# Gating norm and inverse merges cut into smaller pieces, and the later adaLN modulations moved from the chain stage into the projection stage

## The chip, the cores and the metric

The kernel runs on one core of a Trainium2 chip. The metric is the device time of one execution in microseconds. The engines named below: PE (TensorE, matrix products), DVE (VectorE), ACT (ScalarE), POOL (GpSimd) and SP (SyncE, here the queue that issues most transfers).

## The reference, cut to what matters

Two layers work on 512 latent tokens and 256 context tokens of width 1024. Each sub-layer is a norm, a modulation from a conditioning vector (adaLN), a mixer, a norm, a gate and a residual. In the first layer the mixer is a spatial-gating MLP (4 groups) beside a bidirectional RWKV-7 (8 heads), both fed by one projection; the second layer's mixer is an mLSTM; a ConvFFN follows each.

```
def ada_mod(cvec, w, b):                       # w: 1024 x 6144, six vectors of 1024
    m = jax.nn.silu(cvec) @ w + b
def spatial_gate(p, w_s, b_s, g_v):
    u, v = jnp.split(jax.nn.gelu(p[..., :2 * A_WIDTH]), 2, axis=-1)
    v = rmsnorm(v.reshape(bn, t // CHUNK, CHUNK, A_GROUPS, A_GDIM), g_v)
    z = jnp.einsum('gpq,bnqgc->bnpgc', w_s, v) + b_s.T[None, None, :, :, None]
    return u * z.reshape(bn, t, A_WIDTH)
def rwkv7_scan(r, w, k, v, kk, b, s0):
    def step(s, inp):
        sa = jnp.einsum('bhvk,bhk->bhv', s, kk_t)
        s = s * w_t[:, :, None, :] - sa[..., None] * b_t[:, :, None, :] + v_t[..., None] * k_t[:, :, None, :]
        return s, jnp.einsum('bhvk,bhk->bhv', s, r_t)
```

## The kernel before, in words

The change touches the first layer's mixer alone. It is written in three parts.

*Norm and first projections.* The tokens are normed, transposed and modulated with the first two modulation vectors (`ada_0`); the result `hT` is kept as a high and a low half. A matrix product of full precision is three passes: weights high by input high, weights high by input low, weights low by input high.

*Projection stage.* A *unit* is one 128-column tile of the input projection: `load_w` fetches 512 KB of weights into one of two `raw` slots (`strm.raw` is 2), ACT writes the high half, POOL the low half (two buffers each), and `proj_pass` runs 24 passes over the 512 latent tokens and 24 over the 256 context tokens, into PSUM banks 0 and 1. There are 23 units: three for the low-rank inputs, then k, r and v for four tiles `ct` of the RWKV part (`kr`, `v`) and u and v for four groups of the gating part (`sgu`). For every `ct`, `prep_e` makes the decays and key products, `prep_n` the 64x64 matrices of each chunk, and `prep_t` their triangular inverses: a scan of 31 steps on DVE (L597, L599) over 32x32 blocks, then transposes `Td`, `Tn`, `On`, copies on ACT (L613, L614), and two merges on PE (L621 with the ACT copy L624, L630 with the DVE copy L633). The gating norm in `sgu` transposes v on PE (L822), squares it on ACT (L826), takes the power on POOL (L827, L828), multiplies on DVE (L829), multiplies with the spatial weights on PE (L833) and evicts on DVE (L837, L841).

*Chain stage.* The four tiles are written to and read back from HBM, and the chunk recurrence runs as two interleaved lanes over a pair of tiles (`lane`, `chains`), with the next inputs (`preps`), the inverses of tiles 2 and 3 (`Ts`) and the finishing norms beneath it, in six blocks `b`. The remaining modulations of the first layer that need the matrix `ada_w` (`ada_job([1, 2])`: vectors 2, 3 and 4) are computed in blocks 2 to 4 as well: `ada_gen` loads a slab of weights and multiplies it with the two conditioning vectors, in column tiles of 32 of the array (L157), all sums in PSUM bank 7; at the end the sums are copied (L162), transposed (L165) and added to the bias (L169). The result is read first in the gate of the output projection that follows.

All generators are merged by `weave`: a piece is what lies between two `yield`s, a generator with weight n and offset f has its i-th piece at the key f + (1 − f)(i + 0.5)/n, and the smallest key comes next:

```
k = min(range(len(live)), key=lambda j: live[j][3] + (1 - live[j][3]) * (live[j][1] + 0.5) / live[j][2])
```

`part_of(g, n)` takes n pieces of a generator, `part(n)` n pieces of the gating groups. The order so written is the priority for the framework's planner, which sets the order on each engine and puts in the waits; each engine, and the SP queue, then works strictly in its order. The projection stage has three rounds, `ct` = 0, 1, 2: in round `ct` the inverse of tile `ct` (in round 2 the first seven pieces of tile 2's inverse) is woven with `prep_e` and `prep_n` of tile `ct + 1`, and with its v, the k and r of tile `ct + 2` and `NA[ct]` pieces of the gating groups.

Of the kernel before, what the change touches and what calls it, by code (L numbers as in the profile page):

```python
# [74 lines left out]
def _build(ctx, tc, xall, par, cst, ada_0, ada_w, ada_t, w_in, w_out, ffn_up, ffn_down, lora, wsT, a_bs, c_in, c_gate, c_out, mneg, parf, parm, out):  # L75
# [33 lines left out]
    class strm:  # L109
        pool, rawp, raw, hi, lo = None, None, 2, 2, 2  # L110
# [33 lines left out]
    def ada_gen(g, pool, tag, rawb, cols=1024, rtag="araw", width=None):  # L144

        n = min(2048, 5120 - g * 2048)
        width, cols = width or cols, min(cols, n)
        m = n // 512
        pb = bank(f"ada_{g}", tag)
        for kt in range(KT):  # L150
            for c0 in range(0, n, cols):
                pl = pool[(c0 // cols) % len(pool)] if isinstance(pool, list) else pool
                raw = pl.tile([P, width], F32, tag=rtag, name=f"ada{g}{kt}{c0}", bufs=rawb)[:, :cols]
                nc.sync.dma_start(raw, ada_w[kt, :, (g - 1) * 2048 + c0:(g - 1) * 2048 + c0 + cols])
                for q2 in range(cols // 512):
                    q = c0 // 512 + q2
                    nc.tensor.matmul(pb[32 * q:32 * q + 32, :], silu[:, kt, :],  # L157
                                     raw[:, q2 * 512:(q2 + 1) * 512],
                                     start=(kt == 0), stop=(kt == KT - 1))
            yield  # L160
        sb = (pool[0] if isinstance(pool, list) else pool).tile([P, width], F32, tag=rtag, name=f"adasb_{g}", bufs=rawb)[:, :512]
        V.tensor_copy(sb[:32 * m], pb[:32 * m])  # L162
        pt = bank(f"adat_{g}", tag)
        for j in range(4):
            nc.tensor.transpose(pt[:, j * 128:j * 128 + 32 * m], sb[:32 * m, j * 128:(j + 1) * 128], ident[:32 * m, :32 * m])  # L165

        o = PC.at["ada_b0"][0]
        for cnd in range(2):
            V.tensor_tensor(mod[0][:, cnd, g * 16:g * 16 + 4 * m].rearrange("p (q j) -> p q j", q=m),  # L169
                            pt.rearrange("p (j q r) -> p q j r", j=4, q=4)[:, :m, :, cnd],  # L170
                            par_s[:, o + g * 16:o + g * 16 + 4 * m].rearrange("p (q j) -> p q j", q=m), ALU.add)
# [130 lines left out]
    def weave(*gens):  # L302
        for _ in woven(*gens):
            pass

    def part_of(g, n):
        for _ in range(n):
            next(g)
            yield

    def run(gen):
        for _ in gen:
            pass
# [16 lines left out]
    with ExitStack() as lx:  # L330
# [249 lines left out]
        def prep_t(ct, prbank):  # L580

            s = st[ct]
            NF = s["NF"]
            Ai = wkT.tile([P, 32, 32], F32, tag="Ai", name=f"Ai{ct}")
            V.transpose(Ai, NF[:, 0:32].rearrange("p u t -> p t u"))
            Ti = wkT.tile([P, 32, 32], F32, tag="Ti", name=f"Ti{ct}")
            G.memset(Ti, 0.0)
            G.memset(Ti.rearrange("p a b -> p (a b)")[:, 0:1024:33], 1.0)
            for s_ in range(31):
                m = 31 - s_  # L590
                for e, tag, c0, c1 in ((V, "fs", 0, min(s_ + 1, SPLIT)), (G, "fg", SPLIT, s_ + 1)):
                    w = c1 - c0
                    if w < 1:
                        continue
                    tp = wkT.tile([P, 256 if tag == "fs" else FGN], F32, tag=tag, name=f"{tag}{ct}{s_}")
                    tpv = tp[:, :m * w].rearrange("p (a b) -> p a b", b=w)
                    e.tensor_tensor(tpv, Ai[:, s_ + 1:32, s_:s_ + 1].to_broadcast([P, m, w]),  # L597
                                    Ti[:, s_:s_ + 1, c0:c1].to_broadcast([P, m, w]), ALU.mult)
                    e.tensor_tensor(Ti[:, s_ + 1:32, c0:c1], Ti[:, s_ + 1:32, c0:c1], tpv, ALU.add)  # L599
                if s_ % 3 == 2:  # L600
                    yield
            Td = wkT.tile([P, 32, 32], F32, tag="Ai", name=f"Td{ct}")
            Tn = wkT.tile([P, 32, 32], F32, tag="Tn", name=f"Tn{ct}")
            V.transpose(Td, Ti)
            V.transpose(Tn, Ti.rearrange("p t s -> p s t"))
            On = wkT.tile([P, 24, 32], F32, tag="Ti", name=f"On{ct}")
            V.transpose(On, NF[:, 32:56])
            s["TT"] = (fin if ct > 1 else wkS).tile([P, 1536], F32, tag="TT", name=f"TT{ct}")
            TT = c3(s["TT"])
            tdu = Td.rearrange("p t u -> p u t")  # L610
            for b0 in (0, 64):
                G.memset(TT[b0 + 32:b0 + 64, :, 0:32], 0.0)
                A.copy(TT[b0:b0 + 32, :, 0:32], tdu[b0:b0 + 32, 0:24, :])  # L613
                A.copy(TT[b0 + 32:b0 + 64, :, 32:64], tdu[b0 + 32:b0 + 64, 0:24, :])  # L614
            yield
            Wm = wkT.tile([P, 24, 32], F32, tag="Ai", name=f"Wm{ct}")
            for (u0, nu) in ((0, 16), (16, 8)):
                pw = prbank(f"w{ct}{u0}")
                for k in range(nu):
                    for b0 in (0, 64):  # L620
                        mm(pw[b0:b0 + 32, k * 32:k * 32 + 32], On[b0 + 32:b0 + 64, u0 + k, :],  # L621
                           TT[b0 + 32:b0 + 64, u0 + k, 32:64], start=True, stop=True)
                for b0 in (0, 64):
                    A.copy(Wm[b0:b0 + 32, u0:u0 + nu, :], pw[b0:b0 + 32, 0:nu * 32].rearrange("p (u t) -> p u t", t=32))  # L624
                yield
            for (u0, nu) in ((0, 16), (16, 8)):
                pw = prbank(f"t{ct}{u0}")
                for k in range(nu):
                    for b0 in (0, 64):
                        mm(pw[b0:b0 + 32, k * 32:k * 32 + 32], Tn[b0:b0 + 32, :, u0 + k],  # L630
                           Wm[b0:b0 + 32, u0 + k, :], start=True, stop=True)
                for b0 in (0, 64):
                    V.tensor_copy(TT[b0:b0 + 32, u0:u0 + nu, 32:64],  # L633
                                  pw[b0:b0 + 32, 0:nu * 32].rearrange("p (u t) -> p u t", t=32))
                yield
            nc.sync.dma_start(set_part(ct, "TT"), s["TT"])
# [165 lines left out]
                yield  # L802

        def sgu(g):
            role = "7" if g == 3 else "67"
            pl, pcx = unit(g, f"u{g}")
            ug = wkR.tile([P, T], F32, tag="ug", name=f"ug{g}", bufs=1)
            A.activation(ug[:, 0:TC], pcx, AF.Gelu_apprx_tanh)
# [9 lines left out]
            for (t0, nt) in ((0, 2), (2, 4)):  # L818
# [6 lines left out]
                for i in range(nt):  # L825
                    A.activation(vn[:, i * 128:i * 128 + 128], pt[:, i * 128:i * 128 + 128], AF.Square, accum_out=ss[:, i:i + 1])  # L826
                G.tensor_scalar(ss[:, :nt], ss[:, :nt], 1.0 / 128, EPS, ALU.mult, ALU.add)  # L827
                G.tensor_tensor(ss[:, :nt], ss[:, :nt], eps_t[:, 2:3].to_broadcast([P, nt]), ALU.pow)  # L828
                V.tensor_tensor(vn[:, :nt * 128].rearrange("p (a q) -> p a q", q=128), pt[:, :nt * 128].rearrange("p (a q) -> p a q", q=128),  # L829
                                ss[:, :nt].unsqueeze(2).to_broadcast([P, nt, 128]), ALU.mult)  # L830
                pz = bank(f"pz{g}{t0}", role)
# [27 lines left out]
        def chained(*gens):  # L859
            for g in gens:  # L860
                yield from g
# [20 lines left out]
                next(SG)  # L882
                yield

        NA = (4, 6, 6)
        Ts = [prep_t(ct, lambda name: bank(name, "7")) for ct in (2, 3)]
        run(kr(0))
        weave((start_prep(0), 8), (chained(v(0), kr(1), part(0)), 3 + 0))
        run(prep_n(0))
        for ct in range(3):  # L890
            n = NA[ct]
            weave((prep_t(ct, prbank), 13, 0.0) if ct < 2 else (part_of(Ts[0], 7), 7, 0.2), (chained(start_prep(ct + 1), prep_n(ct + 1)), 9 + 3, 0.0),
                  (chained(v(ct + 1), *([kr(ct + 2)] if ct < 2 else []), part(n)), 3 + n, 0.0))
        run(SG)
        ex.close()
        hx.close()
        rx.close()
# [49 lines left out]
            nc.sync.dma_start(t, set_part(ct, "bv"))  # L947
            st[ct]["bv"] = t

        late = {}  # L950

        def inverse():
            yield from Ts[1]
            tx.close()
            late["p"] = lx.enter_context(tc.tile_pool(name="late0", bufs=1))
            nc.scalar.dma_start(lwg, lora[:, 1024:1536])

        def preps(cts, g):
# [14 lines left out]
        for b, (k, g) in enumerate(blocks):  # L973
# [3 lines left out]
                kk_, gg_ = blocks[b + 1]  # L977
                todo.append((preps(pairs[kk_], gg_), 10))
            if b == 0:
                todo.append((chained(Ts[0], part_of(Ts[1], 6)), 14))  # L980
            elif b == 1:
                todo.append((inverse(), 9))
            elif b < 5:
                todo.append((part_of(ada, (5, 6, 5)[b - 2]), (5, 6, 5)[b - 2]))
            if b == 3:
                for ct in range(2):
                    load_bv(ct)
# [5 lines left out]
            weave(*todo)  # L993
            if g < 2:
                run(part_of(C[k], 4))
            if b == 1:
                ada = ada_job([1, 2], late["p"], 2, 2048)
            if b == 2:
                C.append(chains(pairs[1], ys[1]))
            if b == 4:  # L1000
                run(ada)
                gate_rows(0, 0, "7")
                scale_vec(0, 1)
                load_bv(2)
                load_bv(3)
# [606 lines left out]
```

## Time and profile before

| | |
|---|---|
| median of three runs | 1954.63 us (1948.76 to 1961.74) |
| the profiled execution | 1946.71 us, span of the records 1944.9 us |
| busy: PE, DVE, ACT, POOL | 1825.8, 1332.6, 800.8, 305.7 us |
| mean granted clock of PE | 0.97 |
| projection stage, chain stage | about 104 to 366 us, 366 to 612 us of the span |

Busy time counts an engine's instructions on data; a matmul's end is modelled, and matmuls overlap, so a busy PE is not PE at its peak. The line "PEclk" gives the TensorE clock that was granted, in tenths of full speed, in 40 slices of the span. In a table by stretches, each engine has its busy microseconds and, in brackets, its instructions. A line of waits names the engine and line that waited, what it waited for, the total in microseconds, how often, and the longest.

### The profile page before, as it was taken

The numbers are of one execution on the slowest core, as the hardware profiler recorded it, in microseconds if no ns is written. First come the engines' busy times: TensorE is split into PE (matmuls) and PEld (weight loads), VectorE is DVE, ScalarE is ACT, GpSimd is POOL, SyncE is SP. The second block draws the span as 40 slices with busy tenths as digits, with TensorE's granted clock in tenths as the row PEclk, the third lists the DMA queues.
The fourth block names the chain that finished last, engine by engine and source line by source line (L and its number), as shares of the span: only waits on it lengthen the run. The fifth ranks groups of instructions, "written<-read, shape, count | busy, mean of one in ns | idle before, by whom it ended". The sixth has DMA issues, their size and how long they took to land.

```text
span 1944.9 us, 31874 instructions
## 1 busy us (share of the span) xinstructions
PE 1825.8 (94%) x12411; PEld 1501.0 (77%) x12411; DVE 1332.6 (69%) x2669; ACT 800.8 (41%) x1429; POOL 305.7 (16%) x429
## 2 busy tenths in 40 slices
PE   6998789698998999999999998999999989999998
PEld 4777677587756888888888887778888768888886
DVE  4379676857445589999994337667777678777534
ACT  4374645524335542222232226575554343333322
POOL 2222222311000222323330002100110010000001
PEclk9999889889998999999999999999999999999999
DMA  7133121633774534444432224421111312222222
GB/s 296 55 125 125 67 96 65 194 83 93 221 201 137 173 106 158 152 168 163 163 136 77 101 96 163 159 86 44 33 44 44 130 68 98 97 96 95 93 97 87
DMA packets 102887, 227.77 MB, mean 117 GB/s; under 512 B 28224, under 2 KB 44048, under 8 KB 99664
## 3 DMA queue, kind: packets, MB, share of 16 engines
q1 hardware_dynamic: 100976, 222.26, 33.8%
q10 hardware_dynamic: 1760, 3.47, 0.5%
q8 instruction: 98, 1.61, 0.3%
q14 instruction: 53, 0.43, 0.1%
HBM read 199.31 MB, written 26.39 MB: 116 GB/s over the span
## 4 chain that ended last, share of the span: by engine, by line
PE 58%; DVE 2%; ACT 2%; POOL 1%; issue 1%; POOLq 0%; DVEq 0%; ACTq 0%
PE of L1044 5%; PE of L1045 5%; PE of L1043 5%; PE pl_fb L267 4%; PE pl_fb L268 4%; PE pl_fb L266 4%; PE pl_fa L267 4%; PE pl_fa L266 4%; PE pl_fa L268 4%; PE pd L1456 1%; PE pe L1433 1%; PE pc_fb L268 1%; PE pc_fa L268 1%; PE pc_fb L267 1%; PE pc_fa L267 1%; PE pc_fb L266 1%
## 5 line engine op out<-in xcount | busy, mean ns | idle before, releaser
L1091 DVE SCALAR_TENSOR_TENSOR cv<-pl_fa,fpar,cv 128x441 f32<-128x441 f32 (+2 forms) x352 | 243.2, 691 | 15.3 <-ACT cv L1080 10.0
L1045 PE MATMUL of<-hi_fd,hlo 128*128 128x512 f32 x440 | 171.4, 392 | 3.1 <-DVE hlo L1115 3.1
L1044 PE MATMUL of<-lo_fd,hhi 128*128 128x512 f32 x440 | 172.1, 391 | 1.6 <-DVE lo_fd L125 1.6
L1043 PE MATMUL of<-hi_fd,hhi 128*128 128x512 f32 x440 | 171.1, 391 | 0.0
L201 DVE SCALAR_TENSOR_TENSOR aj<-am,srb 128x512 f32<-128x512 f32 x224 | 163.4, 730 | 6.3 <-DMA am<-in_ada_t_dram 1.1
L1115 DVE TENSOR_TENSOR hlo<-hid,hhi 128x512 fp32r<-128x512 f32 (+1 forms) x66 | 39.1, 601 | 128.5 <-ACT hhi L1114 128.3
L1114 ACT ACTIVATE hhi<-hid 128x512 fp32r<-128x512 f32 (+1 forms) x66 | 36.7, 559 | 170.6 <-PE of L1044 167.2
L1045 PEld LDWEIGHTS of<-hi_fd,hlo 128*128 128x128 f32 x440 | 83.2, 189 | 20.7 <-DVE hlo L1115 3.5
L1044 PEld LDWEIGHTS of<-lo_fd,hhi 128*128 128x128 f32 x440 | 82.7, 188 | 19.9 <-DVE lo_fd L125 3.1
L125 DVE TENSOR_TENSOR lo_fd<-raw_fd,hi_fd 128x1024 fp32r<-128x1024 f32 x66 | 80.8, 1224 | 25.0 <-ACT hi_fd L124 24.9
L1043 PEld LDWEIGHTS of<-hi_fd,hhi 128*128 128x128 f32 x440 | 82.8, 188 | 17.9 <-DVE pt_f L1028 0.4
L222 POOL TENSOR_SCALAR rstd_p_f<-sq_f,sq_f 128x1 f32<-128x1 f32 x10 | 7.2, 724 | 557.2 <-ACT jk_f L1022 557.2
L124 ACT ACTIVATE hi_fd<-raw_fd 128x1024 fp32r<-128x1024 f32 x66 | 69.3, 1049 | 27.9 <-DMA raw_fd<-in_ffn_down_dram 11.8
L124 ACT ACTIVATE hi_fa<-raw_fa 128x1024 fp32r<-128x1024 f32 x44 | 46.4, 1055 | 76.3 <-PE pl_fb L267 62.7
L124 ACT ACTIVATE hi_fb<-raw_fb 128x1024 fp32r<-128x1024 f32 x44 | 46.7, 1062 | 68.2 <-PE pc_fa L267 39.0
L125 POOL TENSOR_TENSOR lo_fb<-raw_fb,hi_fb 128x1024 fp32r<-128x1024 f32 x22 | 59.4, 2698 | 88.9 <-ACT hi_fb L124 88.9
L125 POOL TENSOR_TENSOR lo_win<-raw_win,hi_win 128x1024 fp32r<-128x1024 f32 x23 | 57.6, 2508 | 91.2 <-ACT hi_win L124 85.0
L1093 ACT ACTIVATE cv<-cv 128x512 f32<-128x512 f32 x44 | 27.8, 632 | 106.4 <-DVE cv L1091 106.4
L266 PE MATMUL pl_fa<-h0f_lathi,hi_fa 128*128 128x512 f32 x176 | 69.0, 392 | 0.0
L266 PE MATMUL pl_fb<-h0f_lathi,hi_fb 128*128 128x512 f32 x176 | 68.8, 391 | 0.0
L267 PE MATMUL pl_fb<-h0f_latlo,hi_fb 128*128 128x512 f32 x176 | 68.8, 391 | 0.0
L267 PE MATMUL pl_fa<-h0f_latlo,hi_fa 128*128 128x512 f32 x176 | 68.8, 391 | 0.0
(695 smaller groups left out, 5485.5 us busy)
## 6 DMA issues: line engine op xcount, KB each, us to landing
raw_fd<-in_ffn_down_dram SPq DMA_DIRECT2D x66, 512.0 KB, 3.2
am<-in_ada_t_dram SPq DMA_DIRECT2D x112, 256.0 KB, 2.9
raw_fa<-in_ffn_up_dram SPq DMA_DIRECT2D x44, 512.0 KB, 3.3
raw_fb<-in_ffn_up_dram SPq DMA_DIRECT2D x44, 512.0 KB, 3.2
raw_win<-in_w_in_dram SPq DMA_DIRECT2D x23, 512.0 KB, 3.3
ada<-in_ada_dram SPq DMA_DIRECT2D x8, 1024.0 KB, 8.8
ada<-in_ada_w_dram SPq DMA_DIRECT2D x8, 1024.0 KB, 7.0
raw_cin<-in_c_in_dram SPq DMA_DIRECT2D x16, 512.0 KB, 3.5
```

The source lines that it names most:

```text
L124: nc.scalar.activation(hi[:, c], raw[:, c], AF.Copy)
L125: strm.sub.tensor_tensor(lo[:, c], raw[:, c], hi[:, c].bitcast(F32), ALU.subtract)
L201: V.scalar_tensor_tensor(place(f"aj{i}{h}{cnd}", "junk"), raw, 1.0, sb[cnd * 2 + h], ALU.mult, ALU.mult, accum_out=acc[:, cnd, h:h + 1])
L266: mm(p, wh[:, kt, :], hh[:, kt], start=(kt == 0), stop=False)
L267: mm(p, wh[:, kt, :], hl[:, kt], start=False, stop=False)
L268: mm(p, wl[:, kt, :], hh[:, kt], start=False, stop=(kt == KT - 1))
L1043: mm(o[i][hf], hi, w[0][:, c], start=f, stop=False)
L1044: mm(o[i][hf], hi, w[1][:, c], start=False, stop=False)
L1045: mm(o[i][hf], lo, w[0][:, c], start=False, stop=e)
L1091: V.scalar_tensor_tensor(dv, src[:, r0 + dy:r1 + dy, c0 + dx:c1 + dx], fw(ky * 3 + kx), dv, ALU.mult, ALU.add)
L1114: A.activation(hi, hid[cnd][:, k], AF.Copy)
L1115: V.tensor_tensor(lo, hid[cnd][:, k], hi.bitcast(F32), ALU.subtract)
```

## The change

1. `ada_gen` yields after every slab instead of after every row block, and its job now runs in the projection stage: slabs of 1024 columns (512 KB) from the pool and the two slots of the units' `raw` weights, eight pieces in each of the three rounds (16 for job 1, 8 for job 2), its end after the rounds. The pool `late0` and the pieces in the chain stage go.
2. `sgu` yields between the power and the multiply, and keeps all its PSUM tiles in bank 6 (before: banks 6 and 7 in turn, bank 7 alone for group 3). A group has six pieces instead of four; the quotas `NA` become 7, 8, 9.
3. `prep_t` yields between the matmuls and the copies of its merges, 19 pieces instead of 15. Its weight in the rounds becomes 19 instead of 13; in round 2 the seven pieces have weight 12 and no offset (before: 7 and 0.2); the weights in the chain stage grow by four each.

```diff
@@ ada_gen
                     nc.tensor.matmul(pb[32 * q:32 * q + 32, :], silu[:, kt, :], ...
-            yield
+                yield
@@ prep_t, both merges
                         mm(pw[b0:b0 + 32, k * 32:k * 32 + 32], ...
+                yield
                 for b0 in (0, 64):
                     A.copy(Wm[...], ...)            # second merge: V.tensor_copy(TT[...], ...)
@@ sgu
-            role = "7" if g == 3 else "67"
+            role = "6"
...
                 G.tensor_tensor(ss[:, :nt], ss[:, :nt], eps_t[:, 2:3].to_broadcast([P, nt]), ALU.pow)
+                yield
                 V.tensor_tensor(vn[...], pt[...], ss[...], ALU.mult)
@@ the rounds of the projection stage
-        NA = (4, 6, 6)
+        NA = (7, 8, 9)
+        ada = ada_job([1, 2], wkR, strm.raw, 1024, "raw")
...
-            weave((prep_t(ct, prbank), 13, 0.0) if ct < 2 else (part_of(Ts[0], 7), 7, 0.2), (chained(start_prep(ct + 1), prep_n(ct + 1)), 9 + 3, 0.0),
+            weave((prep_t(ct, prbank), 19, 0.0) if ct < 2 else (part_of(Ts[0], 7), 12, 0.0), (part_of(ada, 8), 8, 0.0), (chained(start_prep(ct + 1), prep_n(ct + 1)), 9 + 3, 0.0),
                   (chained(v(ct + 1), *([kr(ct + 2)] if ct < 2 else []), part(n)), 3 + n, 0.0))
         run(SG)
+        run(ada)
@@ the chain stage
-            late["p"] = lx.enter_context(tc.tile_pool(name="late0", bufs=1))
...
-                todo.append((chained(Ts[0], part_of(Ts[1], 6)), 14))
+                todo.append((chained(Ts[0], part_of(Ts[1], 6)), 18))
-                todo.append((inverse(), 9))
-            elif b < 5:
-                todo.append((part_of(ada, (5, 6, 5)[b - 2]), (5, 6, 5)[b - 2]))
+                todo.append((inverse(), 13))
-            if b == 1:
-                ada = ada_job([1, 2], late["p"], 2, 2048)
...
-                run(ada)
```

More of the change, by code (lines that the diff above doesn't have):

```diff
@@ L828, in sgu @@
                 G.tensor_tensor(ss[:, :nt], ss[:, :nt], eps_t[:, 2:3].to_broadcast([P, nt]), ALU.pow)
+                yield
                 V.tensor_tensor(vn[:, :nt * 128].rearrange("p (a q) -> p a q", q=128), pt[:, :nt * 128].rearrange("p (a q) -> p a q", q=128),
@@ L948, in load_bv @@
             st[ct]["bv"] = t
-        late = {}
         def inverse():
```

## The prediction, on record before the changed kernel ran

> **What bounds the kernel now.** I read the page first, for the place of the stages, then windows cut at the stage borders, then who waits for whom in the two stages that the change touches. The page's slices are 48.6 us each.
>
> ```profile
> span 1944.9 us, 31874 instructions
> PE   6998789698998999999999998999999989999998
> DVE  4379676857445589999994337667777678777534
> PEclk9999889889998999999999999999999999999999
> ```
>
> TensorE is the busiest engine, but slices 2 to 12 (97 to 630 us) are the loosest: PE is not at 9 throughout, and the granted clock is 8 in several. That is where the change lies: the projection stage (conv, decay and gating tiles, inverses of tiles 0 and 1, about 104 to 366 us) and the chain stage (366 to 612 us). Columns below: stretch, length, busy us (instructions) of PE, PEld, DVE, ACT and POOL, clock, DMA share, GB/s.
>
> ```profile
> 104.00:366.00 262.00, 227.29 (x1742) 183.77 (x1740) 200.33 (x335) 147.13 (x275) 70.66 (x62) 0.92 0.28 103
> 104.00:196.00 92.00, 82.46 (x524) 65.88 (x522) 82.17 (x125) 50.74 (x80) 25.70 (x18) 0.96 0.34 126
> 196.00:216.00 20.00, 16.30 (x270) 13.01 (x271) 5.33 (x10) 14.42 (x39) 6.59 (x9) 0.83 0.08 29
> 216.00:276.00 60.00, 49.28 (x276) 40.42 (x274) 57.67 (x98) 28.97 (x40) 14.53 (x11) 0.93 0.30 115
> 276.00:310.00 34.00, 33.19 (x381) 28.25 (x380) 7.12 (x13) 20.37 (x45) 11.73 (x11) 0.85 0.17 58
> 310.00:366.00 56.00, 46.05 (x297) 36.21 (x296) 48.04 (x92) 32.63 (x73) 12.11 (x14) 0.93 0.28 108
> 388.00:484.00 96.00, 89.68 (x1690) 76.85 (x1687) 59.27 (x181) 34.14 (x86) 13.19 (x28) 0.88 0.33 90
> 484.00:586.00 102.00, 96.92 (x1553) 67.24 (x1551) 47.02 (x145) 35.02 (x89) 7.14 (x17) 1.00 0.69 203
> ```
>
> The projection stage swings. In 216:276 VectorE is full (57.7 of 60 us) and PE has 10.7 us idle; in 276:310 PE is full (33.2 of 34) and VectorE works 7.1. In the whole stage PE is idle 262 − 227.3 = 34.7 us and VectorE 61.7 us: neither bounds it alone, the order does. The chain stage from 484 to 586 is packed: PE 95%. The waits of the projection stage (104 to 366 us; total, times, longest) say which pieces hold the engines:
>
> ```profile
> PE vt L822 <- ACT vg L813: 13.5, 2, 7.9
> PE pz L833 <- DVE vn L829: 5.3, 4, 2.1
> PE pl_rT L266 <- DVE kT L285: 5.1, 1, 5.1
> DVE vn L829 <- POOL sgss L828: 22.5, 7, 8.6
> DVE TT L633 <- PE t L630: 16.8, 1, 16.8
> ACT TT L613 <- DVE Td L604: 12.0, 2, 7.3
> ```
>
> VectorE, an in-order engine, stood 22.5 us at the gating norm's multiply (its cause, the power on POOL, is in the same piece) and 16.8 us once at the merge's copy (its matmuls are in the same piece). The longest PE wait, 7.9 us, starts with ScalarE: its four TT copies stand ahead of the vg gelu and wait for the inverse's transpose.
>
> **The change part by part.** *Later modulations, chain stage.* The matmuls L157 leave it. What they take there, what they wait for, and one piece of each kind (four column tiles in a 2048-wide piece, two in a 1024-wide one):
>
> ```profile
> 484.00:586.00 102.00, 16.94 (x96) 2.41 (x96) 1.00 0.69 203
> PE ada L157 <- DMA ada<-in_ada_w_dram: 2.4, 3, 1.2
> 501.19 1.06 PE L157 MATMUL ada<-ada,silu 128*32 128x512 f32 x8 [0.34 <-DMA ada<-in_ada_w_dram]
> 578.09 1.05 PE L157 MATMUL ada<-ada,silu 128*32 128x512 f32 x4
> 583.31 0.46 PE L165 MATMUL adat<-cst_s,adasb 64*128 64x64 f32 x4
> ```
>
> Sixteen pieces are 16.94 us of PE in a stretch that is 95% packed, so I take 16.94 × 0.95 = 16.1 us as the gain. Ends: 19.3 us (with the 2.4 us of waits), and 8 us, half, if the two lanes are held by their own steps as much as by PE. For the first end speaks the pace. Columns here: busy us of the lanes' Qs copies L710 and their count:
>
> ```profile
> 388.00:484.00 96.00, 5.49 (x21) 0.88 0.33 90
> 484.00:586.00 102.00, 5.60 (x21) 1.00 0.69 203
> ```
>
> 21 steps take 102 us with the modulations beneath, 4.86 us each, against 4.57 us with the inverses beneath; less 16.1 us it would be 4.09. The tails (two copies, eight transposes, four additions) move too; they are under 3 us on engines with room at either place and I put them at 0 on the path.
>
> *Later modulations, projection stage.* With 1024 columns a piece, job 1 becomes 16 pieces and job 2 stays 8. A two-tile piece takes 1.05 us, as long as a four-tile one, so 24 × 1.05 = 25.2 us of PE arrive where 16.94 left; with two sets of four transposes (0.46 us the narrower set, L165, some 0.8 the wider as an estimate) I count 26.5. PE's demand there is then 227.3 + 26.5 = 253.8 us. The longest well-packed stretch of these two stages is 484:586 with its 95%; at 95% the projection stage would last 253.8 / 0.95 = 267.1 us, **5.1 us longer**. Its cover is the 34.7 us that PE idles; were none of it usable the cost would be 26.5, were all of it −8.2 (a stage of 253.8 us). I take 5.1.
>
> From the weave's key (i + 0.5)/n I worked out where the pieces fall: the 24 loads alternate with the unit loads, except four in a row near the end of the first round and four near the end of the third. They share the two raw slots and SP's queue with the units' weights.
>
> ```profile
> raw_win<-in_w_in_dram SPq DMA_DIRECT2D x23, 512.0 KB, 3.3
> ada<-in_ada_w_dram SPq DMA_DIRECT2D x8, 512.0 KB, 3.9
> 84.95 0.40 PE L266 MATMUL pl_rT<-h_lathi,hi_win 128*128 128x512 f32 x1
> 93.29 0.38 PE L453 MATMUL kkn0b<-sq,cst_s 128*128 128x256 f32 x1
> ```
>
> A load lands in 3.3 to 3.9 us; one unit's 48 passes took 93.29 − 84.95 = 8.3 us. A raw slot that an L157 pair holds until PE gets there leaves the next unit still one split pair (hi and lo have two buffers) ahead, so loads stay covered when the queue moves.
>
> *Gating norm.* A yield after the power, and all its banks in bank 6, since bank 7 holds the modulations' sums. No instruction is added; six pieces a group instead of four, with quotas 7, 8, 9, which brings unit U1 from the second round into the first. What may go is PE's 5.3 us at pz and part of VectorE's 22.5 us. The worst of the latter, 8.6 us, is no order of VectorE's: it has run out of scan work there (5.3 of 20 us busy in 196:216). One bank for vt and pz makes the second half's transposes wait for the first half's last read; at most it gives back the 5.3 us. I put both together at 0, between −5 and +5.
>
> *Merges.* Four yields more, 19 pieces, and the weight 19 in place of 13: the scan's ten pieces fall in the first half of a round instead of the first three quarters, and the merges end inside the round instead of behind everything. The scans come sooner than the conv and decay products, so the products of the next tile come as much later. What this can save is the tails 196:216 and 276:310, where VectorE does 12.5 us in 54; it can cost as much at the head, where VectorE is full already. I expect a shorter tail and a longer head, and credit only 3 us, for the clock: the stage's mean is 0.92, and PE's gap of 7.9 us stands before the 0.83 of 196:216. Ends: −15 (below, first rival) and +5.
>
> **Sum.** −16.1 + 5.1 + 0 − 3 = −14.0 us. Against the profiled execution, 1946.71 us with 1.8 us around its span, that is 1932.7. This execution lies 7.9 us under the median of the runs, 1954.63, against which the change will be measured; so I predict 1954.6 − 14.0 = **1940.6 us**. About 1% (19.5 us) is what a measurement of this kernel tells from no change.
>
> **The rivals.** *First, the stage shrinks too.* The granted clock of 0.92 is 0.08 × 262 = 21 us of PE time; the low values stand beside gaps of 7.9 and 5.1 us. If the fillers close such gaps, some 15 us come back beyond the 3 already counted: −14 − 15 = −29, 1925.6 us. For it: VectorE's 39 us in two waits of the kind that the yields split. Against: 276:310 has 0.85 with PE busy throughout, so filling alone does not make the clock. The Trainium skill, "TensorE: Matmul & The Clock Gate", section "HAM oscillation — how this bites in real kernels", says that a PE idle gap of more than about 3.4 us drops the clock to half and a stretch of steady work restores it; by that rule every closed long gap pays twice, and this rival would be the likeliest. The trace agrees at 196:216 and leaves 276:310 unexplained, so I give it 0.26.
>
> *Second, the other side: PE stands at the ring.* An L157 pair reads its raw slot directly, and PE is in order: everything behind it, units included, waits for a load that stands in SP's queue behind stores that wait for VectorE. In the same stretch the queue's own waits are (total, times, longest):
>
> ```profile
> SPq L816 <- DVE vg L837: 35.9, 3, 12.4
> SPq L577 <- DVE RB L537: 23.9, 3, 10.6
> SPq L550 <- DVE vT L285: 18.6, 3, 14.0
> SPq L550 <- DVE bv L548: 17.9, 2, 12.7
> SPq L636 <- DVE TT L633: 11.7, 1, 11.7
> ```
>
> If a load is caught once behind the longest of each row, PE has one unit of 8.3 us in hand and stands for the rest: 61.4 − 5 × 8.3 = 19.9 us, and 5 × 3.3 = 16.5 us for landings: 36.4. With the 5.1 and no credit for the clock the stage grows 41.5; less 16.1 it is +25.4, **1980.0 us**. It decides once PE stands more than 11 us at such loads in all (30 us for 1%). Against it: in the chain stage the same loads, behind the same kind of queue, cost 2.4 us. Chance 0.18.
>
> *Third, the change does not do what it says.* The program's order is not the engine's: the vT unit of the first round starts on PE before the bon product of the work ahead of it,
>
> ```profile
> 126.36 0.47 PE L266 MATMUL pl_vT<-h_lathi,hi_win 128*128 128x512 f32 x1 [0.86 <-DVE rT L285]
> 128.77 0.48 PE L453 MATMUL bon0b<-bv,cst_s 128*128 128x256 f32 x1 [1.23 <-DVE bv L546]
> ```
>
> so a planner already moves ready work into waits, and a yield may change nothing. With the lanes' low end, −8 + 5.1 = −2.9, 1951.7 us. Chance 0.14.
>
> **How the numbers follow.** The forecast has 0.42; its own range is 1927 to 1957 (chain −19.3 to −8, stage −8 to +10). Faster by over 1% (under 1935.1 us) are nearly all of the first rival and a third of the forecast: 0.40. Slower by over 1% (above 1974.2 us) is most of the second rival: 0.15. Between lies 0.45. The range runs from 1915 (the first rival's 1926 with the 10 us by which the forecast may be off) to 1978, which leaves out half of the second rival and the far end of the first.
>
> **What would show it.** Right: no L157 between 484 and 586, that stretch about 16 us shorter at some 4.1 us a Qs step; 96 L157 instructions between 104 and 366, still at about 1.05 us a pair of tiles; VectorE's waits at L829 and L633 well below 22.5 and 16.8; the stage between 254 and 272 us long. Second rival: PE waiting for the modulation loads or for hi_win for tens of us, SP's waits at L115 and L154 grown. First rival: the stage's clock near 1.00 and its length near 250. The prediction fails above all if the new order makes the head of each round longer by more than its tail gets shorter: then the conv products come late, and with them the next round.

## The result, and the profile after

The changed kernel takes 1938.16 us (median of four runs, 1936.52 to 1940.14) against 1953.29 us (four runs, 1948.76 to 1961.74): a ratio of 0.9925, 95% interval 0.9903 to 0.9948, which is 14.6 us less (10 to 19; the two medians are 15.1 us apart). The forecast was 14.0 us less. The sum came out, but by luck: two of its terms did not, in opposite directions, and a third thing moved that no term named. The rest of this text is about that.

The page of the changed kernel, profiled in an execution of 1936.52 us:

```profile
span 1934.7 us, 31922 instructions
...
PE   6999989878998999999999999999999989999998
...
DVE  4378775867555589999995337667777678777534
...
PEclk9999999989999999999999999999999999999999
```

PE and the clock are a little fuller in slices 2 to 12 than before, and these are still the loosest. To see the time, I cut both traces at the same marks, the stores that SP's queue issues at the ends of the pieces (start in us, length, line). Before, then after:

```profile
216.16 0.35 SPq L636 DMA_DIRECT2D setd<-TT  x1
...
309.95 0.33 SPq L636 DMA_DIRECT2D setd<-TT  x1
...
364.83 0.32 SPq L843 DMA_DIRECT2D mixd<-vg  x1
...
485.89 0.33 SPq L636 DMA_DIRECT2D setd<-TT  x1
...
610.57 0.43 SPq L115 DMA_DIRECT2D raw_mixl<-mixd  x1
```

```profile
218.18 0.32 SPq L638 DMA_DIRECT2D setd<-TT  x1
...
322.73 0.33 SPq L638 DMA_DIRECT2D setd<-TT  x1
...
386.24 0.32 SPq L846 DMA_DIRECT2D mixd<-vg  x1
...
490.70 0.33 SPq L638 DMA_DIRECT2D setd<-TT  x1
...
602.30 0.44 SPq L115 DMA_DIRECT2D raw_mixl<-mixd  x1
```

The first two marks end the inverses of tiles 0 and 1, the third is the last gating store (the end of the projection stage, which I start at 107 us), the fourth ends tile 3's inverse and with it the chain stage's first part, the fifth is the first load of the mixing that follows. So the projection stage went from 257.8 to 279.2 us (+21.4), the chain's first part from 121.1 to 104.5 (−16.6), its second part from 124.7 to 111.6 (−13.1). What lies outside these marks is 1439.4 to 1441.9 us of the span in all fourteen profiles that follow here; nothing else moved. The profiled pair differs by 10.2 us, less than the medians, because the profiled execution of before lies 6.6 us under its median and that of after 1.6 under its own.

The windows of the projection stage, before and after (columns as in the prediction: length, PE, PEld, DVE, ACT, POOL, clock, DMA share, GB/s). The last two rows of after are its tails, as far ahead of the first and the second mark as 196:216 and 276:310 were before:

```profile
107.00:365.00 258.00, 224.29 (x1731) 181.69 (x1729) 196.47 (x329) 144.27 (x269) 67.82 (x62) 0.92 0.28 105
```

```profile
107.00:386.00 279.00, 254.02 (x1836) 184.10 (x1834) 207.62 (x349) 152.19 (x275) 75.05 (x62) 0.96 0.41 142
198.00:218.00 20.00, 20.00 (x323) 13.58 (x322) 8.07 (x15) 11.60 (x36) 5.85 (x7) 0.94 0.66 236
288.70:322.70 34.00, 31.07 (x332) 24.69 (x330) 11.42 (x15) 14.66 (x35) 12.22 (x9) 1.00 0.49 181
```

and of L157, the modulations' product, alone (PE, PEld, clock, DMA share, GB/s):

```profile
107.00:386.00 279.00, 33.26 (x96) 4.33 (x96) 0.96 0.41 142
```

PE's work in the stage is now 254.0 us, or 257.0 from 104 us on, where the forecast of 253.8 starts; L157 takes 33.3 us of it where 25.2 were forecast. The two loose tails are fuller: in the first PE went from 16.30 to 20.00 us and VectorE from 5.33 to 8.07, in the second VectorE from 7.12 to 11.42. And yet 25 us of PE's time stay idle, where the forecast had 13.

The chain stage, by the lanes' Qs copies (length, busy us and count of them, clock, DMA share, GB/s); before cut at its own marks, then after:

```profile
364.83:485.89 121.06, 5.75 (x22) 0.84 0.43 113
485.89:610.57 124.68, 6.92 (x26) 1.00 0.58 172
```

```profile
386.24:490.70 104.46, 5.32 (x20) 0.89 0.49 129
490.70:602.30 111.60, 7.44 (x28) 1.00 0.28 80
491.00:581.00 90.00, 6.38 (x24) 1.00 0.32 90
```

The last row is the stretch where the modulations would lie: 24 steps in 90 us, 3.75 us each, against 4.86 before and 4.09 forecast (by the marks of the whole second part, 3.99 against 4.80). But the first part, which holds no modulation in either kernel, is 16.6 us shorter as well. Of the 48 steps two moved from the first part to the second.

The waits of the projection stage (total, times, longest):

```profile
PE vt L824 <- ACT vg L815: 2.2, 1, 2.2
...
PE pz L836 <- DVE vn L832: 3.7, 3, 2.1
...
PE ada L157 <- DMA ada<-in_ada_w_dram: 1.6, 1, 1.6
...
DVE vn L832 <- POOL sgss L830: 10.6, 5, 4.8
...
DVE TT L635 <- PE t L631: 21.8, 4, 10.1
...
ACT hi_win L124 <- DMA raw_win<-in_w_in_dram: 14.1, 5, 3.9
...
SPq L154 <- PE ada L157: 41.9, 9, 16.9
...
SPq L115 <- PE ada L157: 36.6, 9, 11.8
```

The gating norm's wait fell from 22.5 to 10.6 us, PE's 13.5 us at vt to 2.2. The merge copy's wait did not fall: 21.8 us in four pieces instead of 16.8 in one. The last three rows are new: ScalarE's split of a unit's weights waits for their load, because SP waits for PE to free the raw slots that the modulations now share. SP waited for these slots before as well, 91.4 us for POOL's half of the split; the waits for L157 are what the sharing added.

### The profile page after: what moved, and what is told of

Its sections match the earlier page's. It is cut to its first block, busy times and chain, and to the rows that moved or that the text cites. A ratio compares the mean times of both kernels' runs of the same rounds, so it can differ in the third digit from the quotient of the medians.

```text
span 1934.7 us, 31922 instructions
## 1 busy us (share of the span) xinstructions
PE 1828.7 (95%) x12411; PEld 1493.4 (77%) x12411; DVE 1336.3 (69%) x2669; ACT 806.7 (42%) x1433; POOL 312.1 (16%) x429
## 4 chain that ended last, share of the span: by engine, by line
PE 58%; DVE 2%; ACT 2%; POOL 2%; issue 1%; DMA 1%; POOLq 0%; DVEq 0%; ACTq 0%; SPq 0%
PE of L1041 5%; PE of L1042 5%; PE of L1040 4%; PE pl_fb L267 4%; PE pl_fb L268 4%; PE pl_fb L266 4%; PE pl_fa L267 4%; PE pl_fa L266 4%; PE pl_fa L268 4%; PE pd L1453 2%; PE pe L1430 1%; PE kv L1386 1%; PE pc_fb L268 1%; PE pc_fa L268 1%; PE pc_fb L267 1%; PE pc_fa L267 1%
## 5 line engine op out<-in xcount | busy, mean ns | idle before, releaser
L1088 DVE SCALAR_TENSOR_TENSOR cv<-pl_fa,fpar,cv 128x441 f32<-128x441 f32 (+2 forms) x352 | 243.3, 691 | 15.5 <-ACT cv L1077 10.2
L125 DVE TENSOR_TENSOR lo_fd<-raw_fd,hi_fd 128x1024 fp32r<-128x1024 f32 x66 | 80.8, 1225 | 25.2 <-ACT hi_fd L124 25.1
```

The source lines that it names most:

```text
L125: strm.sub.tensor_tensor(lo[:, c], raw[:, c], hi[:, c].bitcast(F32), ALU.subtract)
L1088: V.scalar_tensor_tensor(dv, src[:, r0 + dy:r1 + dy, c0 + dx:c1 + dx], fw(ky * 3 + kx), dv, ALU.mult, ALU.add)
```

## The experiments

Twelve kernels ran, one of them the kernel before once more; each ratio is against the kernel before, run beside it on the same chip. Where two ratios are subtracted, the interval has the two half-widths added in squares. First the table, because most verdicts are read across it. Stage lengths are in us, cut at the marks above.

| kernel | ratio (95%) | projection | chain, 1st part | 2nd part |
|---|---|---|---|---|
| before | 1 | 257.8 | 121.1 | 124.7 |
| e5: before again (single run) | – | 259.3 | 121.1 | 127.3 |
| after | 0.9925 (0.9903–0.9948) | 279.2 | 104.5 | 111.6 |
| e1: before, no late modulations | 0.9880 (0.9863–0.9897) | 266.7 | 119.9 | 105.5 |
| e2: after, no late modulations | 0.9843 (0.9828–0.9858) | 258.6 | 105.9 | 113.6 |
| e3: yields, no move | 0.9953 (0.9938–0.9968) | 262.1 | 104.7 | 135.9 |
| e4: move (and bank 6) | 0.9942 (0.9928–0.9957) | 281.1 | 105.7 | 113.1 |
| e6: bank 6 alone | 0.9982 (0.9965–0.9998) | 266.5 | 103.9 | 134.6 |
| e11: one transpose earlier | 0.9953 (0.9938–0.9969) | 258.7 | 108.9 | 131.1 |
| e8: after, four tiles | 0.9909 (0.9881–0.9936) | 280.1 | 105.6 | 112.8 |
| e13: e8, products first | 0.9926 (0.9905–0.9947) | 276.9 | 104.2 | 112.9 |
| e9: after, no slab loads | 0.9870 (0.9846–0.9894) | 271.6 | 103.4 | 111.6 |
| e10: after, small products | 0.9882 (0.9854–0.9911) | 273.5 | 101.6 | 113.0 |
| e14: after, no merge yields | 0.9942 (0.9921–0.9962) | 282.0 | 101.9 | 111.5 |

**The modulations left out, at either place (e1, e2).** In the kernel before and in the changed one:

```diff
-                raw = pl.tile(...); nc.sync.dma_start(raw, ...)
-                    nc.tensor.matmul(pb[32 * q:32 * q + 32, :], silu[:, kt, :], raw[...], ...)
                 yield
...
+            V.tensor_copy(mod[0][:, cnd, g * 16:...], par_s[...])
```

> The kernel before without the loads, products and sums of the later modulations (vectors 2 to 4 are left at their bias); the pieces of the weave stay, empty. It prices the modulations in the chain stage. If they cost there what they occupy of PE (16.9 us, 95% packed), the time falls by 16 us or a little more (19 with their waits), all of it between 486 and 587 us, and the 98 us between 388 and 486 stay. If the lanes are held by their own steps, it falls by 8 us or less. If removing them also lets the planner order the first half better, 388 to 486 falls too, by up to 15 us.

> The changed kernel without the loads, products and sums of the later modulations (vectors 2 to 4 left at their bias). It prices them in the projection stage. By the sum of the prediction (PE's demand over a 95% packing) they cost there 5 us, at most 26. The stage grew by some 21 us with the change: if the modulations are the cause, this kernel is 15 to 25 us under the changed one and its three rounds are back near 109, 94 and 55 us; if the pieces' new order is the cause, it is under it by 5 us or less and the rounds stay near 111, 105 and 63.

e1 gains 23 us (20 to 27), nearly all in the second part of the chain: 124.7 or 127.3 becomes 105.5. Its first part keeps the length of before. So the modulations cost the chain over 20 us, and the first part's −16.6 us is not theirs. e2 against the changed kernel is 0.9925 − 0.9843 = 0.0082, 16 us (11 to 21): what they cost at the new place. Its row:

```profile
107.00:366.00 259.00, 232.83 (x1730) 185.82 (x1728) 196.18 (x335) 150.79 (x273) 70.12 (x62) 0.91 0.28 104
```

PE idles 26.2 us in this row and 25.0 us in that of the changed kernel: in these two profiles the modulations filled, on balance, hardly any of PE's idle time.

**Yields without the move, and the move without the yields (e3, e4).** e3 is the changed kernel with the modulations back in the chain stage; e4 is the kernel before with them in the rounds, the yield after every slab, and the gating tiles in bank 6, which they need.

```diff
# e3, against after
-            weave((prep_t(ct, prbank), 19, 0.0) ..., (part_of(ada, 8), 8, 0.0), (chained(...
+            weave((prep_t(ct, prbank), 19, 0.0) ..., (chained(...
+                todo.append((part_of(ada, (5, 6, 5)[b - 2]), (5, 6, 5)[b - 2]))
# e4, against before
+            role = "6"
+        ada = ada_job([1, 2], wkR, strm.raw, 1024, "raw")
+            weave((prep_t(ct, prbank), 13, 0.0) ..., (part_of(ada, 8), 8, 0.0), (chained(...
```

> All of the change but the move: the modulations are again in blocks 2 to 4 of the chain stage, the new pieces, weights, quotas and the single bank for the gating norm stay. Theory A (the move alone matters): the time is that of before within 5 us, with 98 and 101 us in the halves of the chain stage. Theory B (the merges' pieces made the first half of the chain stage shorter): 388 to 486 is 83 us as in the changed kernel, the second half 101, and the time 10 to 15 us under before.

> The move alone: the modulations in the rounds as in the change and the single bank 6 for the gating norm, but the pieces, weights and quotas of before. Theory A: the time of the changed kernel within 5 us, the first half of the chain stage at 83 us, the rounds 20 us longer than before. Theory B: the first half of the chain stage stays at 98 us, the second falls to 90, the rounds grow by some 20, and the time is that of before or up to 10 us more.

Neither theory holds: the chain's first part is about 105 us in both, with the new pieces and without them. Whatever shortened it is in each half of the change.

**The kernel before again, and bank 6 alone (e5, e6).** e5 is the kernel before, unchanged.

```diff
# e6, against before
-            role = "7" if g == 3 else "67"
+            role = "6"
```

> The kernel before once more, for its profile. Its projection stage took 257.9 us in the profile of before and 266.8 us in the kernel without the modulations, whose engine order up to there is the same, line by line. If the stage varies from one execution to the next, this profile lies between 258 and 268 us there while the chain stage repeats within 2 us (121 and 125 us); if the difference came from the modulations in some other way, it is 258 again.

> The kernel before with one edit: the gating norm's PSUM tiles all in bank 6. In its engine order the transpose On of tile 2's inverse stands ahead of the memsets of the chain's buffers on VectorE, as it does in the changed kernel; in the kernel before it stands behind them. Theory On (this place decides when tile 2's merges can start): the stretch from the last gating store to the store of tile 3's inverse falls from 121 to about 105 us, and the time by 5 to 10 us, since the second half gives some of it back. Theory move (that stretch fell because the modulations left, their slots and their bank with them): it stays at 121 and the time within 3 us.

e5 repeats the first part at 121.1 us. e6, one line about the banks of tiles that are finished before that part begins, has it at 103.9, and gives 7 to 10 us of that back in the second part (134.6 against 127.3 and 124.7); the whole gains 3.5 us (0.4 to 6.8). Reading VectorE's timelines for what stands otherwise at the start of the first part, one instruction stood out: On, the transpose of tile 2's inverse that its merges need. Before (VectorE, then the first merge on PE):

```profile
371.35 1.76 DVE L914 MEMSET rbp<- 128x2048 f32 x1 [0.38 <-DMA LB<-setd]
...
386.21 0.98 DVE L607 STREAM_TRANSPOSE On<-NF 128x768 f32<-128x768 f32 x1
...
390.98 0.24 PE L621 MATMUL w<-TT,On 32*32 32x32 f32 x2
```

After:

```profile
379.06 0.98 DVE L607 STREAM_TRANSPOSE On<-NF 128x768 f32<-128x768 f32 x1
...
388.82 0.28 PE L621 MATMUL w<-TT,On 32*32 32x32 f32 x2 [3.74 <-ACT TT L614]
...
389.62 1.76 DVE L919 MEMSET rbp<- 128x2048 f32 x1 [3.13 <-DMA mixd<-vg]
```

And with bank 6 alone, its last gating store first:

```profile
373.50 0.32 SPq L843 DMA_DIRECT2D mixd<-vg  x1
...
376.48 0.98 DVE L607 STREAM_TRANSPOSE On<-NF 128x768 f32<-128x768 f32 x1
...
377.82 0.28 PE L621 MATMUL w<-TT,On 32*32 32x32 f32 x2 [5.87 <-POOL rbp L914]
377.84 1.76 DVE L914 MEMSET rbp<- 128x2048 f32 x1 [0.38 <-issue]
```

Before, the first merge starts 26.2 us after the last gating store (364.83); after, 2.6 us after it (386.24); in e6 4.3 us after it (373.50). Before, the On transpose stands behind the memsets of the chain's buffers and the copies out of the first chain products. The merges wait for it, and tile 3's inverse, in the same buffers, for the merges.

**That one transpose alone (e11).** The kernel before, with the planner told that this transpose is urgent, for tile 2 only:

```diff
-            V.transpose(On, NF[:, 32:56])
+            with crit(400 if ct == 2 else 0):
+                V.transpose(On, NF[:, 32:56])
```

> The kernel before with one edit: the transpose On of tile 2's inverse is given a higher priority, which puts it ahead of all but one of the chain's memsets on VectorE; the order before it is unchanged. Theory On: the stretch from the last gating store to tile 3's store falls from 121 to about 106 us, the time by 5 to 10 us. Theory move: nothing changes beyond 3 us.

```profile
372.26 1.76 DVE L915 MEMSET rbp<- 128x2048 f32 x1 [0.38 <-DMA LB<-setd]
...
373.95 0.91 DVE L608 STREAM_TRANSPOSE On<-NF 128x768 f32<-128x768 f32 x1
...
375.17 0.28 PE L622 MATMUL w<-TT,On 32*32 32x32 f32 x2 [11.15 <-issue]
```

The projection stage is untouched (258.7 us), the first part falls to 108.9, the second rises to 131.1, and the whole gains 9.2 us (6 to 12). So the place of a transpose of 0.98 us is what shortened the first part. This is shown for the place together with what the planner builds on it: behind the transpose the merges and the chain's own pieces come in another order too. Why the planner put it where it did in each kernel is not shown. The clock is not the cause: the first part has 0.84 before and 0.89 after, but 0.83 in e6, which is as short there as the changed kernel.

**Four column tiles a slab (e8).** The changed kernel with each slab's 1024 columns multiplied in four tiles of 256 instead of two of 512.

```diff
-                for q2 in range(cols // 512):
-                    nc.tensor.matmul(pb[32 * q:32 * q + 32, :], silu[:, kt, :], raw[:, q2 * 512:...], ...)
+                for q in range(4):
+                    nc.tensor.matmul(pb[32 * q:32 * q + 32, c0 // 4:c0 // 4 + 256], silu[:, kt, :], raw[:, q * 256:...], ...)
```

> The changed kernel with each 1024-column slab of modulation weights multiplied in four column tiles of 256 columns instead of two of 512; the result is the same. The L157 work is then some 0.65 us a slab instead of 1.05 to 1.4 (24 slabs, 33 us of PE busy now), about 16 us in all. If the modulations cost their PE time in the projection stage, the stage gets 10 to 16 us shorter and the time 8 to 15 us less than the changed kernel's. If they cost by where they stand (waits, order of the units), it stays within 4 us.

The product's own row in the stage, then all engines there, and ScalarE's wait for the units' weights:

```profile
107.00:388.00 281.00, 23.12 (x192) 5.23 (x192) 0.90 0.41 142
```

```profile
107.00:388.00 281.00, 252.03 (x1923) 190.75 (x1922) 205.68 (x353) 152.62 (x274) 72.23 (x60) 0.90 0.41 142
```

```profile
ACT hi_win L124 <- DMA raw_win<-in_w_in_dram: 21.4, 7, 6.0
```

The busy time fell from 33.3 to 23.1 us, and nothing that can be measured followed: 280.1 us for the stage, a ratio whose interval overlaps that of the changed kernel. The Trainium skill, "TensorEngine Tiling (Array Packing)", section "Theoretical Speedup", gives four column tiles of 32 up to four times the speed of one; the busy time shows part of that step, from two to four tiles, the kernel's time nothing of it. ScalarE's wait grew, from 14.1 to 21.4 us. And the clock fell, from 0.96 to 0.90: the rest of PE's work took 228.9 us (252.0 − 23.1) where it had taken 220.8 (254.0 − 33.3), which is 8 of the 10 us. The four executions of e8 list a clock of 0.968 to 0.975 over the whole span, those of the changed kernel 0.977 to 0.980. Whether the shorter products lower the clock was not tested.

**The ring or PE (e9, e10).** Does a modulation piece cost its product's time on PE, or the raw slot and the transfer that it takes from the units? e9 keeps the products and drops the loads; e10 keeps the loads, multiplies 32 of each 512 columns and leaves out the final transposes.

```diff
# e9, against after
-                raw = pl.tile(...); nc.sync.dma_start(raw, ada_w[...])
+                raw = lw[:, :cols]
# e10, against after
-                    nc.tensor.matmul(pb[32 * q:32 * q + 32, :], silu[:, kt, :], raw[:, q2 * 512:(q2 + 1) * 512], ...)
+                    nc.tensor.matmul(pb[32 * q:32 * q + 32, 0:32], silu[:, kt, :], raw[:, q2 * 512:q2 * 512 + 32], ...)
```

> The changed kernel without the loads of the modulation slabs: the products, as many and as long, read a tile that is there already (vectors 2 to 4 come out as other numbers). Theory ring (the slabs hold the two raw slots and SP's queue, so the units' weights come late): the projection stage falls from 279 us to 259 to 265, ScalarE's waits for the units' weights (14.1 us in the changed kernel) vanish, and the time falls by 12 to 18 us. Theory PE (the products' own time lengthens the stage): it stays within 4 us of the changed kernel.

> The changed kernel with all the slabs loaded, but of each only 32 of 512 columns multiplied and the final transposes left out (vectors 2 to 4 are left at their bias). Theory ring: the stage stays near 279 us and the time within 5 us of the changed kernel. Theory PE: the stage falls to some 262 us and the time by 12 us or more.

```profile
107.00:379.00 272.00, 251.36 (x1842) 185.41 (x1840) 207.62 (x352) 151.15 (x275) 72.18 (x62) 0.95 0.27 101
```

```profile
107.00:380.00 273.00, 242.20 (x1832) 194.10 (x1830) 202.48 (x345) 155.65 (x277) 73.28 (x62) 0.88 0.43 146
```

```profile
ACT hi_win L124 <- DMA raw_win<-in_w_in_dram: 20.3, 5, 6.8
```

Without the loads the kernel gains 0.9925 − 0.9870, 10.7 us (4 to 17), and ScalarE's wait for the units' weights is gone; PE still does 251.4 us of work in the stage, packed to 92%. With the loads and hardly any product it gains 8.4 us (1 to 15); PE's work falls by 12 us and ScalarE still waits, 20.3 us. Neither is the whole 16 us. Both theories are half right, and the intervals are too wide to tell which half is the larger.

**Products ahead of the other work (e13).** e8 with a higher priority on the modulations' products, so that the slots come free sooner.

```diff
+                with tc.high_priority(offset=300):
+                    for q in range(4): ...
```

> The changed kernel with the slabs in four column tiles, as before, and the products at a higher priority, so that a slab leaves its raw slot as soon as PE can take it. Theory ring: the units' weights come earlier, the stage falls by 5 to 12 us and the time to 1926 to 1932 us. If the slots were not what holds the units, it is the four-tile kernel's time within 3 us; if the products now break into the units at bad places, it is slower than that by up to 5 us.

```profile
ACT hi_win L124 <- DMA raw_win<-in_w_in_dram: 6.4, 2, 3.2
PE ada L157 <- DMA ada<-in_ada_w_dram: 10.5, 6, 2.7
```

The wait fell to 6.4 us, the stage to 276.9, and the time is that of the changed kernel (0.9926). But PE's own wait for the slabs rose from 1.6 to 10.5 us: the wait went from ScalarE to PE. So the run does not show that the shared slots cost nothing.

**Without the merges' yields (e14).** The changed kernel without its two new yields in `prep_t` and with the old weights:

```diff
# prep_t, both merges
-                yield
# the rounds (and in the chain stage 14 and 9 for 18 and 13)
-            weave((prep_t(ct, prbank), 19, 0.0) ...
+            weave((prep_t(ct, prbank), 13, 0.0) ...
```

> The changed kernel without the merges' four yields and with the inverse's old weights (13, 14, 9). By the prediction (their worth between a loss of 5 and a gain of 15 us, 3 taken for them and the clock) the time rises by 0 to 5 us. If the yields are what put the transpose On of tile 2 ahead of the memsets, it falls behind them here, the stretch to tile 3's store rises from 105 to about 120 us, and the time by 5 to 8 us; if the order has other causes too, that stretch stays.

0.9942 against 0.9925: 3.3 us slower at the middle, with intervals that overlap. Its first round lasts 124.2 us and its second 96.4, against 111.2 and 104.6 in the changed kernel: the pieces shift work between rounds more than they save any. Their worth is not settled: between a gain of 9 us and a loss of 3. The chain's first part stays at 101.9 us with On still ahead of the memsets, so it is not the merges' yields alone that put On there.

## Why the prediction was right, and where it was not

*The chain, −16.1: mis-sized.* The table divides by two things: whether the modulations lie in the chain, and whether On stands ahead of the memsets. Means of the two parts:

| | On behind | On ahead |
|---|---|---|
| modulations in the chain | 121.1 + 126.0 (before, e5) | 105.8 + 133.9 (e3, e6, e11) |
| moved or left out | 119.9 + 105.5 (e1) | 104.1 + 112.5 (after and seven others) |

Down either column the modulations cost 21.7 or 23.1 us. That is above the end of 19.3 which I gave the term. The step that failed was multiplying 16.94 us by the 0.95 of the packing: their whole demand lay on the path. The product's 16.94, the 2.4 of waits and the under 3 us of the tails, which I had put at 0, add up to 22.3; that they make the price together is reckoned, not shown. The timed runs agree with the price: 23 us (20 to 27) in e1.

*Across the table, a term that was missing.* On's place gives 15 to 16 us in the first part and takes 7 to 8 back in the second, where the one to three of 48 steps that no longer fit the first part are done, at about 4 us each. Net −7.4 or −8.8 us by the marks, −9.2 by e11's time; e1 and e2, which have no modulations and otherwise differ by the whole change, are 7.2 us apart (3 to 12). The forecast had nothing for it. The sign could not be read from the page: no instruction of that part is added or taken out by the change, only the order moves.

*The projection stage, +5.1: mis-sized.* PE's demand came out only 3.2 us above the forecast (257.0 against 253.8), but by luck in its parts: L157 took 33.3 us, not 25.2, and the other work 4.9 us less, at a clock of 0.96 where the forecast had counted it at 0.92. L157 took longer mostly because other work falls between the two tiles of a pair: in the rows below a pair (x4) takes 1.05 us, and each tile alone (x2) 1.04; 13 of the 48 tiles stand alone so. The failed step is the packing. I borrowed 95% from the chain stage; the projection stage reached 254.0/279 = 91%, after 224.3/258 = 87%. At 91% the forecast's 253.8 us make a stage of 279 us, 17 more than 262, and the timed runs give the term as 16 us (11 to 21, e2). By the marks it is 279.9 against 261.4 us, the mean of five profiles with the modulations there against seven without. Why the stage packs at 91% stays open.

```profile
142.90 1.05 PE L157 MATMUL ada<-ada,silu 128*32 128x512 f32 x4
...
345.60 1.04 PE L157 MATMUL ada<-ada,silu 128*32 128x512 f32 x2
347.67 1.04 PE L157 MATMUL ada<-ada,silu 128*32 128x512 f32 x2
```

*The gating norm, 0, and the merges, −3.* e3 has every yield and no move: −9.2 us (6 to 12), of which On's place alone gives as much in e11. What is left for the pieces and the single bank together is about nothing. They may be two effects that cancel: e6, with the single bank and On ahead but no new pieces, is 5.7 us (1 to 10) slower than e3, and as much slower than e11. I was right that the norm's wait would fall (22.5 to 10.6) and that its pieces and bank together are worth about 0, and wrong that the merge copy would wait well below 16.8 us. The tails did become fuller, as forecast, but the 3 us credited for the clock are not shown: with all the pieces and without the modulations there, the stage's clock is 0.90 (e3) and 0.91 (e2), against 0.92 before.

*The sum.* With what the runs show: −22 for the chain, −8 for On, +16 for the stage is −14, where −14.6 was measured. The forecast's −16.1 + 5.1 − 3 is the same number with other terms. It was right in total by luck: what I underrated on both sides of the move partly cancelled, and the rest came from a transpose.

*The first rival*, that the stage shrinks by the clock, failed. I had given the Trainium skill's rule (TensorE: Matmul & The Clock Gate, "HAM oscillation — how this bites in real kernels") that an idle gap of PE of more than about 3.4 us drops the clock, and had written that it leaves 276:310 unexplained. That was a misreading, since the window begins where a gap ends. In the kernel before, PE waited 5.6 us at vt just ahead of it:

```profile
268.00:275.00 7.00, 2.09 (x11) 1.20 (x9) 6.49 (x17) 1.13 (x1) 0.00 (x0) 1.00 0.00 0
275.00:285.00 10.00, 9.28 (x54) 7.76 (x55) 3.73 (x7) 7.32 (x17) 1.89 (x4) 0.50 0.12 42
```

So both tails agree with the rule, and in the changed kernel both gaps at vt (7.9 and 5.6 us, now 2.2 in all) are closed and the clock of the tails is higher: 0.94 instead of 0.83, 1.00 instead of 0.85. Such gaps are not the only cause: from 408 to 425 us the kernel before ran at 0.50 though PE was busy throughout, and in the 7 us ahead of it too. And over the whole stage the yields gave no clock: without the modulations (e2) ScalarE holds PE at vt for 1.9 us only, yet the clock is 0.91 and the stage no shorter than before. The 0.96 came with the modulations' products (one profile each): without the loads it is 0.95 (e9), with the loads and hardly any product 0.88 (e10). Why is not shown.

*The second rival* was right in its mechanism and wrong in its victim. The loads do collide at the ring: SP waits 41.9 and 36.6 us for L157 to free slots, ScalarE 14.1 us for the units' weights. PE itself stood only 1.6 us at a modulation load, far from the 11 us at which it would have decided; only with the products put first (e13) did that wait come near it, at 10.5. *The third*, that nothing happens, fell with the counts: all 96 L157 are in the projection stage.

## What to carry to other kernels

Moving work from a packed stage into the idle time of a loose one pays only the difference in packing: here 22 us left, 16 came back. The best stage's packing of 95% priced the arrival at 5 us and the receiving stage's own 87% would have priced it at about 30 (26.5/0.87 = 30.5); the measured 16 lies between, so give both as the ends of the term. Count the buffers and queue slots that the work takes as well as the engine. When a stretch changes that the edit does not touch, compare the order of the in-order engines there first: a short instruction that others wait for, standing behind memsets, can be worth as much as the rest of the edit, and giving it priority in the kernel before tells whether it is.

## What was not expected

- One VectorE transpose of 0.98 us, moved from 21 us behind the last gating store to somewhere between 8 us ahead of it and 8 us behind, changes the time by 9.2 us (6 to 12, e11) and the part after it by 12 to 17 us (e11, e6). A change of PSUM banks elsewhere (e6) is enough to move it.
- The projection stage differs between executions of one instruction order: before, e5, e1 and e11, alike there, have 257.8, 259.3, 266.7 and 258.7 us. The granted clock goes with it: 0.92, 0.93, 0.90 and 0.93, and PE's work took 224.3 us before and 232.4 in e1. A stage length from one profile is good to about 9 us, so the +21.4 of the single pair above says less than the 16 us of the timed runs.
- Making the modulations' products shorter (e8: 33.3 to 23.1 us busy) and making the weights come sooner (e13: 14.1 to 6.4 us of waits) each gained nothing that could be measured, while leaving either part out altogether gained 8 to 11 us. In e8 the clock was lower, and in e13 PE itself waited more. What holds the stage stays open.
